# A two-layer trunk on one core: the first units' DMA sums begun with the sub-layer, and each plain tile's weights requested one tile ahead

## The chip, the cores and the metric

The kernel runs on one core of a Trainium2 chip. The metric is device time in microseconds (us) of one execution. The engines are TensorE (PE, matmuls), VectorE (DVE), ScalarE (ACT), GpSimd (POOL) and SyncE (SP, which only issues DMAs here). Each engine works off its own instructions in order; semaphores make one wait for another.

## The reference

A decoder trunk of two layers on a sequence of 512 tokens with 1024 channels. Each layer has a feed-forward part (FFN), a mixer of three groups of heads, a second FFN and a gated per-layer embedding:

```python
for i in range(DEPTH):
    h = rmsnorm(x, g_ffn1_pre[i])
    x = x + 0.5 * rmsnorm(swiglu(h, w1_gate[i], w1_up[i], w1_down[i]), g_ffn1_post[i])
    h = rmsnorm(x, g_mix_pre[i])
    # three head groups from h @ w_in[i], concatenated
    mixed = jnp.concatenate([y_sb, y_mla, y_cv], axis=-1) @ w_out[i]
    x = x + rmsnorm(mixed, g_mix_post[i])
    h = rmsnorm(x, g_ffn2_pre[i])
    x = x + 0.5 * rmsnorm(swiglu(h, w2_gate[i], w2_up[i], w2_down[i]), g_ffn2_post[i])
    h = rmsnorm(x, g_ple_pre[i])
    e = jax.nn.sigmoid(h @ w_ple_gate[i]) * (p[i] @ w_ple_proj[i])
    x = x + rmsnorm(e, g_ple_post[i])

def swiglu(x, w_gate, w_up, w_down):
    return (jax.nn.silu(x @ w_gate) * (x @ w_up)) @ w_down
```

All tensors are 32-bit floats. The FFN's inner width is 2816.

## The kernel before, in words

**Products.** Every 32-bit weight tile is cut into a high half `wh` (a cast by ACT, line 267) and a low half `wl` (a difference, line 268, by DVE or POOL), as the activations are (`xh`, `xl`). A product is three matmuls per 128 rows of depth (lines 283 to 285). Both steps stand in `halves`; `load_raw` (line 258) asks SP for the raw tile. Raw tiles without a tag of their own share four buffers, so a load waits until the halves of an earlier tile have read its buffer.

**An FFN.** The inner width is 22 tiles m. The first four are computed plainly: `order` lists eight products (m, j), j = 0 for gate and 1 for up, called order[0] to order[7] here. Each has 24 matmuls of 512 columns and a PSUM bank whose kind `PLAIN_BANKS = "zsfzzsdf"` names. There is one bank of kind f: order[2] has it first, order[7] next. `activate(m)` reads the banks: line 737 multiplies the gate's by the norm's factor `rb`, line 738 is SiLU on ACT, line 739 multiplies by the up result. The first three products are made together with the sub-layer before (`state.products`), the fourth in `more`, the others in the loop that calls `one`.

**The norm's factor.** It is not known when the products start, so it is applied to their results. `Squares` and `Rstd.add` sum the squares (PE, line 386, into `st`), `rsqrt_cols` (line 366, nine small DVE steps from `r_v` to `rt`) takes the reciprocal root, PE transposes it (line 399), and ACT copies it into `rb` (line 400). `state.behind` is the last of the nine steps; ahead of order[6], `state.row()` puts the transposes into PE's order.

**Units.** The other 18 tiles are `Unit`s: seven products of half the width, from sums of weight blocks, in place of eight. `b11`, `b21` and `b22` are blocks of the weights; `t1` and `t3` are differences of two blocks, stored so that a sum makes them: an SP load of one block, and an accumulating DMA issued by POOL (line 666) that adds the other. They have a buffer of their own kind, as `b21` has. `PREPARE` gives each step of a unit a time in product slots:

```python
PREPARE = (
    ("load", "t1", -18), ("load", "t3", -15), ("load", "b11", -11), ("load", "b21", -10), ("load", "b22", -9), ...
```

`prepare(slot)` issues what is due. The inputs of the units (`fh`, `fl`, lines 611 to 631) are made on ACT and DVE while the plain products run.

**What sets the order.** On PE, in the FFN's loop, the order is the one written. On the other engines a scheduler places each instruction by its priority and a modelled time; `tc.issue_after(x)` keeps what is issued under it behind instruction x. Before, the loads and halves of order[6] and order[7], and all of the units' steps that fall into the loop over the plain products, are under `issue_after(state.behind)`.

Of the kernel before, what the change touches and what calls it, by code (L numbers as in the profile page):

```python
# [24 lines left out]
NF = DFF // P  # L25
# [54 lines left out]
HID_WHOLE = "s" * 2 + "a" * 12 + "s" * 8  # L80
# [5 lines left out]
PLAIN = 4  # L86
# [3 lines left out]
PREPARE = (  # L90
    ("load", "t1", -18), ("load", "t3", -15), ("load", "b11", -11), ("load", "b21", -10), ("load", "b22", -9), ("halve", "b11", -5), ("halve", "b21", -4), ("halve", "t1", -3), ("halve", "t2", -2), ("halve", "b22", 1), ("halve", "t3", 0), ("halve", "t4", 7),
)
# [3 lines left out]
ROW_BEFORE = 6  # L96

TRIG_AT = 2
PLAIN_BANKS = "zsfzzsdf"
BANKS = {"z": 3, "s": 2, "v": 1, "d": 1, "f": 1}  # L100
DENSE = 'zfdszzs'
# [54 lines left out]
def hybrid_trunk(ctx: ExitStack, tc: tile.TileContext, a: dict, out: bass.AP):  # L156
# [7 lines left out]
    ps = ctx.enter_context(tc.tile_pool(name="ps", bufs=1, space=PSUM))  # L164

    def slot(dt=F32, name="s", tag="s"):
        return sp.tile([P, S], dt, tag=tag, name=name, bufs=SLOTS[tag])
# [6 lines left out]
    def bank(name="ps", tag=None):  # L174
        if tag is None:
            tag = dense[0][turn[0] % len(dense[0])]
            turn[0] += 1
        return ps.tile([P, S], F32, tag=tag, name=name, bufs=BANKS[tag])
# [62 lines left out]
    def load_w(src, slabs, cols, on="vv", tag=None):  # L241


        per = S // cols
        return [w for k0 in range(0, slabs, per)
                for w in halves(load_raw(src[:, k0:min(k0 + per, slabs)], cols), on[k0 // per % len(on)], tag)]
# [41 lines left out]
    def start():  # L288
# [5 lines left out]
        def part(k):  # L294
            g = gain(0, "ffn1_pre", k)
            h, lo = xs[k]
            A.activation(out=h, in_=x[k], func=AF.Copy, scale=g)
            V.scalar_tensor_tensor(out=lo, in0=x[k], scalar=g, in1=f(h), op0=ALU.mult, op1=ALU.subtract)
# [11 lines left out]
        for k, c in ((4, 0), (6, 1)):  # L310
# [3 lines left out]
            part(k + 1)  # L314
        first = [(w[t, 0] + w[t, 1], bank("ps", PLAIN_BANKS[t])) for t in range(3)]
        for k in range(NK):
# [54 lines left out]
    class Rstd:  # L371
# [3 lines left out]
        def __init__(self, dim, cols=slice(0, S), tag="v", eps=None, keep=None):  # L375
            self.dim, self.blocks, self.st, self.tag = dim, blocks(cols), None, tag
            self.kw = dict(eps=eps if eps is None else eps[:, cols.start // P:cols.stop // P], keep=keep)
# [35 lines left out]
    def blocks(cols):  # L413
        return [slice(c, c + P) for c in range(cols.start, cols.stop, P)]
# [228 lines left out]
    class Unit:  # L643
# [7 lines left out]
        PAIRS = {"t1": ("b12", "b11"), "t3": ("b12", "b22")}  # L651
        SUMS = {"t2": ("t1", "b22"), "t4": ("t2", "b21")}

        def __init__(self, src, forms, z, tag):
            self.src, self.forms, self.z, self.tag = src, forms, z, tag
            self.raw, self.w, self.bank = {}, {}, {}

        def part(self, n):
# [59 lines left out]
    def ffn(l, idx, state, nxt, xtag="s", early=None):  # L718


        xs = state.xs
        hid, late, banks = [], [], {}
        order = [(m, j) for m in range(PLAIN) for j in range(2)]
        src = a[f"w{idx + 1}_gu"]

        def weights(m, j, on="vv"):
            return load_w(src[l, m, j], NK, P, on)

        def hidden(h):
            if len(hid) < EARLY_HID:  # L730
                hid.append(split(h, HID_HALVES[len(hid)]))
            else:
                late.append(h)

        def activate(m):
            g1 = slot(name="g1", tag=HID_WHOLE[m])
            V.tensor_tensor(out=g1, in0=banks[m, 0], in1=rb, op=ALU.mult)  # L737
            A.activation(out=g1, in_=g1, func=AF.Silu)
            V.tensor_tensor(out=g1, in0=banks[m, 1], in1=g1, op=ALU.mult)
            hidden(g1)  # L740

        def one(m, j):
            w, b = weights(m, j), bank("ps", PLAIN_BANKS[2 * m + j])
            product(b, w, xs)
            banks[m, j] = b

        def more():
            for i in range(FIRST, FIRST + MORE):
                with state.later():
                    w = weights(*order[i])  # L750
                banks[order[i]] = bank("ps", PLAIN_BANKS[i])
                product(banks[order[i]], w, xs)

        if l == 0 and idx == 0:
            first, done = state.first, FIRST
            round_constants()
        else:
            first = [(weights(*t, on), bank("ps", b))
                     for t, on, b in zip(order[:FIRST], (ON_FFN1, ON_FFN2)[idx].split(), PLAIN_BANKS)]
            state.products(first, more)  # L760
            done = FIRST + MORE
        for t, (_, b) in zip(order, first):
            banks[t] = b
        forms = input_forms(l, f"ffn{idx + 1}_pre", xs, xtag)
        units = [Unit(src[l, m], forms, "df"[m % 2], HID_WHOLE[m]) for m in range(PLAIN, NF)]
        todo = sorted((7 * i + t, k, i, n, op) for i in range(len(units)) for k, (op, n, t) in enumerate(PREPARE))

        def prepare(slot):
            while todo and todo[0][0] <= slot:
                _, _, k, form, op = todo.pop(0)  # L770
                getattr(units[k], op)(form)

        rb = None
        with tc.manual_schedule(engines={T.engine}):
            for i in range(done, len(order)):
                if i == ROW_BEFORE:
                    rb = state.row()
                with tc.issue_after(state.behind) if i >= ROW_BEFORE else nullcontext():
                    one(*order[i])
                with tc.issue_after(state.behind):  # L780
                    prepare(8 * (i + 1 - len(order)))
                if rb is not None and i % 2:
                    for m in range(len(hid) + len(late), (i + 1) // 2):
                        activate(m)
            for i in range(len(units) + 1):
                for j, (n, back) in enumerate(PRODUCTS):
                    prepare(7 * i + j)
                    if 0 <= i - back < len(units):
                        u = units[i - back]
                        if n == "p4":  # L790
                            hidden(u.p4(rb))
                        else:
                            getattr(u, n)()
        hid += [split(h, t) for h, t in zip(late, HID_HALVES[EARLY_HID:])]
        turn[0] += 2 * NF + (l + idx > 0)

        sq, ys = Squares(), {}

        def down(m):
            return [w for k0, k1 in DOWN_CHUNKS  # L800
                    for w in load_w(a[f"w{idx + 1}_down"][l, m, :, k0:k1, :], k1 - k0, P)]

        together = [bank() for _ in range(TOGETHER)]
        for k0, k1 in DOWN_CHUNKS:
            for c0 in range(k0, k1, 4):
                c1 = min(c0 + 4, k1)
                ws = [load_w(a[f"w{idx + 1}_down"][l, m, :, c0:c1, :], c1 - c0, P) for m in range(TOGETHER)]
                for k in range(c0, c1):
                    for w, o in zip(ws, together):
                        product(o, w[k - c0:k - c0 + 1], hid[k:k + 1], k == 0, last=k == NF - 1)  # L810
        for m in range(NK - LAST_DOWN):
            if early is not None and m == TRIG_AT:
                early()
            if m < TOGETHER:
                o = together[m]
            else:
                o = bank()
                product(o, down(m), hid)
            ys[m] = slot(name="y")
            sq.add(o)  # L820
            V.tensor_copy(out=ys[m], in_=o)
        last = range(NK - LAST_DOWN, NK)
        w = {m: down(m) for m in last}

        def compute(m, c, tick=lambda: None):
            o = bank()
            product(o, w[m], hid, cols=c, tick=tick)
            return o

        for m in last:  # L830
            ys[m] = slot(name="y")

        def evac(m, c, o):
            V.tensor_copy(out=ys[m][:, c], in_=o[:, c])

        return finish(ys, sq, last, compute, evac, lambda k: half[:, l, idx, k:k + 1], nxt, AT_DOWN, eps=state.eps)
# [484 lines left out]
    state = start()  # L1321
    for l in range(DEPTH):
        state = ffn(l, 0, state, (l, "mix_pre"), xtag="m" if l else "s", early=None if l else trig)
        state = mixer(l, state, (l, "ffn2_pre"))
        state = ffn(l, 1, state, (l, "ple_pre"))
        state = ple(l, state, (l + 1, "ffn1_pre") if l + 1 < DEPTH else None)
# [58 lines left out]
```

## Time and profile before

| what | value |
|---|---|
| median of 3 runs | 2171.48 us (2168.61 to 2175.36) |
| profiled execution | 2170.57 us |
| its span in the profile | 2168.8 us |
| mean granted TensorE clock | 0.977 |
| busy: DVE, ACT, POOL | 1549.2, 1116.5, 509.6 us |

The span is the time from the first to the last instruction that the profile shows. In rows of a timeline stand the start in us, the duration, the engine, the line, the operation, what it writes and reads, how many instructions were joined, and in brackets the idle time ahead of it and what ended that. In rows of windows stand the stretch, its length, then busy time and number of instructions of PE, of its weight loads, of DVE, ACT and POOL, then the granted clock, the DMA engines' busy share and GB/s. Rows of the chain of waits have start, duration and what ran.

### The profile page before, as it was taken

The page shows a single profiled execution, that of the slowest core. Times are in us where ns is not written, and L with a number is a line of the kernel's source. Part 1 is how long each engine was busy: PE and PEld are TensorE (multiplying, and loading weights), DVE is VectorE, ACT ScalarE, POOL GpSimd, SP SyncE. Part 2 cuts the span into 40 slices and gives each one's busy share as a digit, 9 for nine tenths or more (in the row PEclk, how much of TensorE's full clock was granted, in tenths as well). Part 3 has the DMA queues.
Part 4 walks back from the last instruction along what each step waited for, and adds up shares of the span by engine and source line. Part 5 has one row for each costly group of instructions (what it writes and reads, how often), then busy time and mean ns, then how long its engine had stood idle before and what let it go on. Part 6 is the DMA issues. An engine that isn't in the chain of part 4 may idle for free.

```text
span 2168.8 us, 35923 instructions
## 1 busy us (share of the span) xinstructions
PE 2070.1 (95%) x13264; PEld 1883.4 (87%) x13264; DVE 1549.2 (71%) x2851; ACT 1116.5 (51%) x2296; POOL 509.6 (23%) x498
## 2 busy tenths in 40 slices
PE   7999999999998999999979999999999989999996
PEld 6999988887887999888869998888878879998886
DVE  7888654778877788636787786257788778785376
ACT  6555533555555556524555555235455555564243
POOL 3111013126432111003331110031263421110043
PEclk9999999999999999999999999999999899999998
DMA  7677332311115775332247763323111157753322
GB/s 213 173 181 175 86 107 67 95 55 52 53 48 137 188 179 146 102 97 79 78 122 189 178 163 93 100 63 99 55 53 47 45 150 195 175 138 102 97 70 67
DMA packets 139425, 244.73 MB, mean 113 GB/s; under 512 B 15600, under 2 KB 26096, under 8 KB 139248
## 3 DMA queue, kind: packets, MB, share of 16 engines
q1 hardware_dynamic: 117792, 204.00, 30.8%
q0 software_dynamic: 20736, 37.76, 11.0%
q8 instruction: 104, 1.70, 0.3%
q10 hardware_dynamic: 720, 0.67, 0.1%
q14 instruction: 73, 0.60, 0.1%
HBM read 240.27 MB, written 2.10 MB: 112 GB/s over the span
## 4 chain that ended last, share of the span: by engine, by line
PE 81%; DVE 13%; ACT 2%; DMA 2%; issue 1%; POOL 0%; SPq 0%; DVEq 0%; ACTq 0%; POOLq 0%
PE ps L283 10%; PE ps L284 10%; PE ps L285 9%; PE ux L684 6%; PE ux L683 6%; PE ux L682 6%; PE uy L684 3%; PE uy L683 3%; PE uy L682 3%; DVE x L571 3%; PE in L283 2%; PE in L284 2%; PE in L285 2%; DVE xl L467 2%; DVE wl L268 2%; PE uz L684 2%
## 5 line engine op out<-in xcount | busy, mean ns | idle before, releaser
L268 DVE TENSOR_TENSOR wl<-raw,wh 128x512 fp32r<-128x512 f32 (+2 forms) x893 | 601.8, 689 | 416.7 <-ACT wh L267 364.1
L267 ACT CAST wh<-raw 128x512 fp32r<-128x512 f32 (+1 forms) x934 | 548.6, 605 | 606.8 <-PE ps L284 273.9
L441 POOL TENSOR_TENSOR sq<-sq 128x256 f32<-128x256 f32 (+1 forms) x165 | 175.5, 1064 | 798.0 <-ACT sq L431 793.4
L284 PE MATMUL ps<-l,wh 128*128 128x512 f32 (+1 forms) x824 | 302.7, 367 | 0.2 <-DVE l L196 0.2
L285 PE MATMUL ps<-h,wl 128*128 128x512 f32 (+1 forms) x824 | 301.9, 367 | 0.0
L283 PE MATMUL ps<-h,wh 128*128 128x512 f32 (+1 forms) x824 | 300.3, 368 | 0.0
L666 POOL DMA_DIRECT2D raw<-in_w_gu x144 | 125.7, 928 | 634.8 <-DVE wl L268 195.3
L684 PE MATMUL ux<-fh,wl 128*128 128x256 f32 x864 | 244.5, 283 | 0.0
L683 PE MATMUL ux<-fl,wh 128*128 128x256 f32 x864 | 244.5, 283 | 0.0
L682 PE MATMUL ux<-fh,wh 128*128 128x256 f32 x864 | 244.4, 283 | 0.0
L283 PE MATMUL ps<-xh,wh 128*128 128x256 f32 (+1 forms) x536 | 176.7, 353 | 36.5 <-DVE g L737 29.0
L284 PE MATMUL ps<-xl,wh 128*128 128x256 f32 (+1 forms) x536 | 184.0, 351 | 13.0 <-DVE xl L467 12.8
L285 PE MATMUL ps<-xh,wl 128*128 128x256 f32 (+1 forms) x536 | 182.6, 346 | 0.0
L284 PEld LDWEIGHTS ps<-l,wh 128*128 128x128 f32 x824 | 155.6, 189 | 25.7 <-DVE l L196 0.8
L285 PEld LDWEIGHTS ps<-h,wl 128*128 128x128 f32 x824 | 155.4, 189 | 25.1 <-DVE wl L268 0.5
L283 PEld LDWEIGHTS ps<-h,wh 128*128 128x128 f32 x824 | 155.5, 189 | 24.5
L682 PEld LDWEIGHTS ux<-fh,wh 128*128 128x128 f32 x864 | 165.8, 192 | 0.5
L683 PEld LDWEIGHTS ux<-fl,wh 128*128 128x128 f32 x864 | 165.8, 192 | 0.5
L684 PEld LDWEIGHTS ux<-fh,wl 128*128 128x128 f32 x864 | 165.8, 192 | 0.0
L283 PEld LDWEIGHTS ps<-xh,wh 128*128 128x128 f32 x536 | 106.1, 205 | 49.3 <-issue 30.6
L284 PEld LDWEIGHTS ps<-xl,wh 128*128 128x128 f32 x536 | 108.9, 204 | 26.9 <-DVE xl L467 16.7
L285 PEld LDWEIGHTS ps<-xh,wl 128*128 128x128 f32 x536 | 108.8, 204 | 10.8 <-DVE wl L268 0.7
(335 smaller groups left out, 5101.7 us busy)
## 6 DMA issues: line engine op xcount, KB each, us to landing
raw<-in_w_gu SPq DMA_DIRECT2D x424, 256.0 KB, 4.2
raw<-in_w_down SPq DMA_DIRECT2D x160, 256.0 KB, 2.6
raw<-in_w_gu POOLq DMA_DIRECT2D x144, 256.0 KB, 5.2
raw<-in_win_f SPq DMA_DIRECT2D x60, 256.0 KB, 2.7
raw<-in_ple_gate SPq DMA_DIRECT2D x32, 256.0 KB, 2.7
raw<-in_wo_a SPq DMA_DIRECT2D x18, 256.0 KB, 2.7
raw<-in_w_down SPq DMA_DIRECT2D x32, 128.0 KB, 2.2
raw<-in_wo_b SPq DMA_DIRECT2D x12, 256.0 KB, 2.7
```

The source lines that it names most:

```text
L267: A.copy(out=h, in_=raw)
L268: (G if on == "g" else V).tensor_tensor(out=lo, in0=raw, in1=f(h), op=ALU.subtract)
L283: T.matmul(oc, wh, xh[:, cols], start=first and k == 0, stop=False, **kw)
L284: T.matmul(oc, wh, xl[:, cols], start=False, stop=False, **kw)
L285: product.last = T.matmul(oc, wl, xh[:, cols], start=False, stop=last and k == n - 1, **kw)
L441: G.tensor_tensor(out=self.acc[:, c], in0=self.acc[:, c], in1=self.last[:, c], op=ALU.add)
L467: iv = V.scalar_tensor_tensor(out=lo, in0=x[k][:, c], scalar=g, in1=f(h), op0=ALU.mult, op1=ALU.subtract)
L571: V.scalar_tensor_tensor(out=x[k][:, c], in0=ys[k][:, c], scalar=gcol(k), in1=x[k][:, c], op0=ALU.mult, op1=ALU.add)
L666: G.dma_start(out=self.raw[n], in_=self.part(m), accum_op=ALU.add)
L682: T.matmul(o, wh, xh, start=first and k == 0, stop=False, **kw)
L683: T.matmul(o, wh, xl, start=False, stop=False, **kw)
L684: T.matmul(o, wl, xh, start=False, stop=k == 3, **kw)
```

## The change

Three edits, all in `ffn` and `Unit`. The units are made when the sub-layer starts, before its first plain products; for the first two (`AHEAD`) t1 and t3 are loaded at once, four SP loads and four accumulating DMAs of POOL, and taken out of the list of things due. In the loop, the weights (loads and halves) of the next plain tile are requested before the product of this one. And these requests are no longer held behind `state.behind`; the units' other steps still are. A unit gets its inputs (`forms`) later. No computation is added or removed. Lines 98 to 655 of before stand two lower in the changed file, the lines of `activate` too.

```diff
+AHEAD = 2
...
-        def __init__(self, src, forms, z, tag):
-            self.src, self.forms, self.z, self.tag = src, forms, z, tag
+        def __init__(self, src, z, tag):
+            self.src, self.z, self.tag = src, z, tag
...
-        def one(m, j):
-            w, b = weights(m, j), bank("ps", PLAIN_BANKS[2 * m + j])
+        def one(m, j, w):
+            b = bank("ps", PLAIN_BANKS[2 * m + j])
             product(b, w, xs)
             banks[m, j] = b
...
+        units = [Unit(src[l, m], "df"[m % 2], HID_WHOLE[m]) for m in range(PLAIN, NF)]
+        todo = sorted((7 * i + t, k, i, n, op) for i in range(len(units)) for k, (op, n, t) in enumerate(PREPARE)
+                      if op != "load" or i >= AHEAD or n not in ("t1", "t3"))
+        for u in units[:AHEAD]:
+            u.load("t1")
+            u.load("t3")
...
-        units = [Unit(src[l, m], forms, "df"[m % 2], HID_WHOLE[m]) for m in range(PLAIN, NF)]
-        todo = sorted((7 * i + t, k, i, n, op) for i in range(len(units)) for k, (op, n, t) in enumerate(PREPARE))
...
+        for u in units:
+            u.forms = forms
         rb = None
         with tc.manual_schedule(engines={T.engine}):
+            ws = [weights(*order[done])]
             for i in range(done, len(order)):
                 if i == ROW_BEFORE:
                     rb = state.row()
-                with tc.issue_after(state.behind) if i >= ROW_BEFORE else nullcontext():
-                    one(*order[i])
+                if i + 1 < len(order):
+                    ws.append(weights(*order[i + 1]))
+                one(*order[i], ws[i - done])
                 with tc.issue_after(state.behind):
                     prepare(8 * (i + 1 - len(order)))
```

Three places show how instructions move; all are in layer 0's second FFN.

SP, the loads around order[6] and order[7], before. raw_7753 and raw_7759 are order[6]'s, raw_7796 and raw_7800 are b11 and b22 of the first unit, raw_7743 to raw_7868 the first blocks of t1 and t3 of three units, raw_7805 and raw_7811 order[7]'s, raw_7798 is b21:

```order
L258 DMA raw_7753<-in_w2_gu 128x512
L258 DMA raw_7759<-in_w2_gu 128x512
L258 DMA raw_7796<-in_w2_gu 128x512
L258 DMA raw_7800<-in_w2_gu 128x512
L258 DMA raw_7743<-in_w2_gu 128x512
...
L258 DMA raw_7868<-in_w2_gu 128x512
L258 DMA raw_7805<-in_w2_gu 128x512
L258 DMA raw_7811<-in_w2_gu 128x512
L258 DMA raw_7798<-in_w2_gu 128x512
L258 DMA raw_7855<-in_w2_gu 128x512
```

SP with the change. raw_7302 to raw_7311 are t1 and t3 of two units, raw_7730 and raw_7736 order[6]'s, raw_7774 and raw_7780 order[7]'s, raw_7846 and raw_7868 t1 and t3 of the third unit, raw_7811 and raw_7815 are b11 and b22, raw_7813 is b21:

```order
L260 DMA raw_7302<-in_w2_gu 128x512
...
L260 DMA raw_7311<-in_w2_gu 128x512
...
L260 DMA raw_7730<-in_w2_gu 128x512
L260 DMA raw_7736<-in_w2_gu 128x512
L260 DMA raw_7774<-in_w2_gu 128x512
L260 DMA raw_7780<-in_w2_gu 128x512
L260 DMA raw_7846<-in_w2_gu 128x512
L260 DMA raw_7868<-in_w2_gu 128x512
L260 DMA raw_7811<-in_w2_gu 128x512
L260 DMA raw_7815<-in_w2_gu 128x512
...
L260 DMA raw_7940<-in_w2_gu 128x512
L260 DMA raw_7813<-in_w2_gu 128x512
```

The four loads have gone up by some ten rows, ahead of the plain tiles, order[7]'s stand straight behind order[6]'s, and b11, b22 and b21 come after them; b21 is behind raw_7940, which waits for b11's halves.

DVE, from the root's first steps to the op that reads order[2]'s bank f (ps_7340, last row), before. wl_7756 and wl_7762 are order[6]'s low halves, wl_7808 and wl_7814 order[7]'s, wl_7843 b11's, wl_7852 b21's, wl_7858 t1's:

```order
L366 TENSOR_SCALAR r_v_7586<-st_7580 128x4
...
L366 TENSOR_SCALAR r_y0_7587<-r_v_7586 128x4
...
L366 SCALAR_TENSOR_TENSOR rt_7585<-r_w_7590,r_z_7589 128x4
L268 TENSOR_TENSOR wl_7756<-raw_7753,wh_7755 128x512
L268 TENSOR_TENSOR wl_7762<-raw_7759,wh_7761 128x512
L268 TENSOR_TENSOR wl_7808<-raw_7805,wh_7807 128x512
L737 TENSOR_TENSOR g1_7875<-ps_7314,rb_7746 128x512
...
L268 TENSOR_TENSOR wl_7814<-raw_7811,wh_7813 128x512
L268 TENSOR_TENSOR wl_7843<-raw_7796,wh_7842 128x512
...
L268 TENSOR_TENSOR wl_7852<-raw_7798,wh_7851 128x512
L268 TENSOR_TENSOR wl_7858<-raw_7743,wh_7857 128x512
...
L737 TENSOR_TENSOR g1_7883<-ps_7340,rb_7746 128x512
```

DVE with the change. wl_7733 and wl_7739 are order[6]'s, wl_7777 and wl_7783 order[7]'s, wl_7843, wl_7852 and wl_7858 are b11's, b21's and t1's again; rt_7597 is the root's last step, and ps_7352 order[2]'s bank:

```order
L270 TENSOR_TENSOR wl_7733<-raw_7730,wh_7732 128x512
...
L270 TENSOR_TENSOR wl_7739<-raw_7736,wh_7738 128x512
L270 TENSOR_TENSOR wl_7777<-raw_7774,wh_7776 128x512
L368 TENSOR_SCALAR r_v_7598<-st_7592 128x4
L270 TENSOR_TENSOR wl_7783<-raw_7780,wh_7782 128x512
...
L368 SCALAR_TENSOR_TENSOR rt_7597<-r_w_7602,r_z_7601 128x4
L270 TENSOR_TENSOR wl_7843<-raw_7811,wh_7842 128x512
L739 TENSOR_TENSOR g1_7891<-ps_7705,rb_7767 128x512
L739 TENSOR_TENSOR g1_7875<-ps_7326,rb_7767 128x512
...
L270 TENSOR_TENSOR wl_7852<-raw_7813,wh_7851 128x512
L270 TENSOR_TENSOR wl_7858<-raw_7302,wh_7857 128x512
...
L739 TENSOR_TENSOR g1_7883<-ps_7352,rb_7767 128x512
```

The four low halves of order[6] and order[7] have moved from behind the root to ahead of its end, and two of `activate`'s first multiplications ahead of b21's half; ahead of the one that reads order[2]'s bank stand b21's and t1's halves.

POOL, before: the mixer's last low half (kl_4796), its squares (sq), and then the accumulating DMAs of the units:

```order
L187 TENSOR_TENSOR kl_4796<-kf_6481,kh_4795 64x512
L441 TENSOR_TENSOR sq_6964<-sq_6964,sq_6966 128x256
...
L441 TENSOR_TENSOR sq_7248<-sq_7248,sq_7250 128x256
...
L666 DMA raw_7743<-in_w2_gu 128x512
L666 DMA raw_7790<-in_w2_gu 128x512
L666 DMA raw_7793<-in_w2_gu 128x512
L666 DMA raw_7802<-in_w2_gu 128x512
L666 DMA raw_7846<-in_w2_gu 128x512
```

POOL with the change:

```order
L189 TENSOR_TENSOR kl_4796<-kf_6481,kh_4795 64x512
L668 DMA raw_7302<-in_w2_gu 128x512
L668 DMA raw_7305<-in_w2_gu 128x512
L668 DMA raw_7308<-in_w2_gu 128x512
L668 DMA raw_7311<-in_w2_gu 128x512
L443 TENSOR_TENSOR sq_6964<-sq_6964,sq_6966 128x256
...
L443 TENSOR_TENSOR sq_7248<-sq_7248,sq_7250 128x256
...
L668 DMA raw_7846<-in_w2_gu 128x512
```

Four of the accumulating DMAs now stand ahead of the mixer's last squares instead of behind them.

## The prediction

> **What bounds the kernel now.** I read the shares of the engines first, then what TensorE (PE) waits for, then PE's rows in order of time, and at each long gap the chain of waits.
>
> ```profile
> PE 2070.1 (95%) x13264; PEld 1883.4 (87%) x13264; DVE 1549.2 (71%) x2851; ACT 1116.5 (51%) x2296; POOL 509.6 (23%) x498
> ```
>
> PE is busy 95% of 2168.8 us, and the change neither adds nor takes away a matmul. So it can only win the rest: places where PE stands, and places where PE runs slowly. The view of waits has one PE entry that is four single waits, and PE's rows in order of time give them:
>
> ```profile
> PE ps L283 <- DVE g L737: 29.0, 4, 8.9
> ...
> 55.02 0.77 PE L283 MATMUL ps<-xh,wh 128*128 128x512 f32 x1 [4.24 <-DVE g L737]
> 692.60 0.76 PE L283 MATMUL ps<-xh,wh 128*128 128x512 f32 x1 [8.89 <-DVE g L737]
> 1134.01 0.77 PE L283 MATMUL ps<-xh,wh 128*128 128x512 f32 x1 [7.26 <-DVE g L737]
> 1771.96 0.76 PE L283 MATMUL ps<-xh,wh 128*128 128x512 f32 x1 [8.59 <-DVE g L737]
> ```
>
> There is one per FFN; I call them stalls 0 to 3. All four stand before the last plain product, order[7], which goes to bank f, held until line 737 has read order[2]'s result. They sum to 28.98 us. Each also costs clock afterwards:
>
> ```profile
> 700.46 0.39 PE L285 MATMUL ps<-xh,wl 128*128 128x512 f32 x1
> 700.69 0.28 PE L682 MATMUL ux<-xh,wh 128*128 128x256 f32 x1
> 62.80 0.28 PE L682 MATMUL ux<-xh,wh 128*128 128x256 f32 x1
> 1141.62 0.28 PE L682 MATMUL ux<-xh,wh 128*128 128x256 f32 x1
> 1779.73 0.28 PE L682 MATMUL ux<-xh,wh 128*128 128x256 f32 x1
> 694.00:696.00 2.00, 2.00 (x6) 1.60 (x5) 2.00 (x5) 1.78 (x4) 0.00 (x0) 0.50 0.00 0
> ```
>
> The granted clock (third number from the right) is 0.50 behind the stall. At the end of the product the matmuls start 0.23 us apart again (700.46 to 700.69); at that pace the 24 matmuls of order[7] need 5.52. They took 8.09 in stall 1 (692.60 to 700.69), and 7.78, 7.61 and 7.77 in stalls 0, 2 and 3: 2.6 + 2.3 + 2.1 + 2.2 = 9.2 us more. All that the change can win here is therefore 29.0 + 9.2 = 38.2 us.
>
> Who ends stall 1? The chain of waits there:
>
> ```profile
> 665.15 0.60 DVE wl L268
> ...
> 666.15 0.60 DVE wl L268
> ...
> 675.57 1.22 DVE wl L268 x2
> 676.86 8.76 DMA raw<-in_w_gu
> 685.64 1.14 ACT wh L267 x2
> 686.80 1.28 ACT L738
> 688.10 0.64 ACT g L738
> ...
> 691.85 0.61 DVE g L737
> ```
>
> Halves of order[6], queued behind the norm's reciprocal root, run at 675.57 and free two raw buffers; order[7]'s weights go into those, and the second landed 8.76 us later. Its cast stands on ScalarE (ACT) ahead of the SiLU work, its difference on VectorE (DVE) ahead of line 737. So PE does not wait for order[7]'s weights as such, but for DVE and ACT work queued behind them. Stall 3 repeats this chain with one number changed, and stalls 0 and 2 have the same links:
>
> ```profile
> 1756.43 8.55 DMA raw<-in_w_gu
> ```
>
> **The change part by part, on stall 1.** *Weights one tile ahead.* order[7]'s loads now follow order[6]'s on SyncE (SP) and wait for order[5]'s halves, 665.15 and 666.15 above. They go out at about 665.8 and 666.8, where b11 and b22 went; before, it was 676.24:
>
> ```profile
> 665.78 2.27 SPq L258 DMA_DIRECT2D raw<-in_w_gu  x4
> 676.24 2.16 SPq L258 DMA_DIRECT2D raw<-in_w_gu  x3
> 677.64 0.60 PE L399 MATMUL rb<-ident,rt 128*128 128x128 f32 x4
> raw<-in_w_gu SPq DMA_DIRECT2D x424, 256.0 KB, 4.2
> raw<-in_w_down SPq DMA_DIRECT2D x160, 256.0 KB, 2.6
> ```
>
> They land by 671 to 672 (median 4.2), while DVE still makes input forms: hidden. The price: four halves, two of order[6] and two of order[7], now stand ahead of the root instead of behind it. 4 x 0.60 = 2.4 us, so the root is done at about 678.0 instead of 675.57. Before, PE's transposes of it ran at 677.64; now they wait 0.4 us.
>
> *What is late next.* On DVE the op that frees bank f (line 739 of the changed file, whose lines here are two higher) is now behind b11's and b21's halves. b21's load stands on SP behind a load that waits for b11's halves, and those follow the root (678.0 + 0.6). b21 goes out near 679.4; before it was the third of the issues at 676.24. With the median of 4.2 it lands at 683.6; cast 0.6, two differences 1.2, line 198 0.6, line 739 0.6, 0.1 to PE: order[7] starts at 686.7. The SiLU branch is ready sooner: transposes and copy to 679.3, then a table load of 1.28 and two SiLUs of 0.64 to 681.9. Against 692.60 that is 5.9 us won. PE was free at 692.60 - 8.89 = 683.7, now 684.1, so 2.6 us of stall stay. The landing is bounded by 2.6 (w_down's median, a quieter stretch) and 8.76 (order[7]'s own before): order[7] at 685.1 or 691.3, 7.5 or 1.3 won. I take 4.2, the same tensor on the same queue.
>
> *The DMA sums first.* Per FFN four SP loads and four accumulating DMAs of POOL leave the crowded stretch. In stages 1 and 3 they are put ahead of the mixer's last squares on POOL, which stands idle there, four issues at some 0.93 us being 3.7 us:
>
> ```profile
> 619.53 2.37 POOL L441 TENSOR_TENSOR sq<-sq 128x256 f32<-128x256 f32 x3 [40.38 <-ACT sq L431]
> L666 POOL DMA_DIRECT2D raw<-in_w_gu x144 | 125.7, 928 | 634.8 <-DVE wl L268 195.3
> 640.00:660.00 20.00, 18.50 (x125) 17.26 (x125) 19.35 (x40) 12.81 (x32) 12.96 (x16) 0.91 0.08 27
> ```
>
> Hidden by those 40 us; without that cover it would be 3.7. The last window before the crowded stretch has a DMA share of 0.08, so the loads find room.
>
> *Stall 3* has stage 1's order; its chain was 0.2 us shorter from load to product: 5.7 won, 2.5 left.
>
> *Stall 2.* Here PE's transposes came later than the root:
>
> ```profile
> 1117.54 1.22 DVE wl L268 x2
> 1120.68 0.60 PE L399 MATMUL rb<-ident,rt 128*128 128x128 f32 x4
> 1067.70 1.01 PE L386 MATMUL st<-con,sq 128*128 128x1 f32 x4 [1.47 <-ACT sq L522]
> ```
>
> Root at 1117.5 + 2.4 = 1119.9, no wait for PE; b11's halves to 1120.5, b21 out at 1121.4, landed 1125.6, then 3.1 us of the same steps: 1128.7 against 1134.01, 5.3 won. PE is free at 1126.75, so 2.0 us stay. The four POOL issues sit among the squares of the sub-layer before, 3.7 us in all; PE's sums over the squares waited until 1067.70 for a square of ACT anyway. I count nothing; the ends are 0 and 3.7 lost.
>
> *Stall 0.* The added loads go ahead of order[3]'s in the first 15 us, and DVE does the moved halves beside POOL's squares:
>
> ```profile
> 24.00:32.00 8.00, 8.00 (x37) 6.64 (x36) 6.36 (x8) 7.48 (x15) 8.00 (x7) 1.00 1.00 268
> 34.42 6.74 POOL L441 TENSOR_TENSOR sq<-sq 128x512 f32<-128x512 f32 x4
> 36.80 1.50 DVE L187 TENSOR_TENSOR fl<-xg,fh 128x512 fp32r<-128x512 f32 x1 [0.20 <-ACT fh L616]
> 44.42 0.16 DVE L366 SCALAR_TENSOR_TENSOR rt<-r_w,r_z 128x4 f32<-128x4 f32 x1
> ```
>
> The root moves from 44.4 to about 45.5, b21 goes out at 46.7, lands at 50.9, and six steps (cast, two differences, lines 741, 674, 198 and 739: 4.2 us) end at 55.1 against 55.02: nothing won. Bounds: four halves at 1.5 instead of 0.6 beside POOL lose 3.6; no wait at all wins 4.2 and 2.3 of clock. The row at 36.80 (1.50, where a difference at 665.15 took 0.60) says that the contention is real. The page "SBUF — State Buffer" of the Trainium skill, section "Who interferes with whom", has it as a rule: VectorE's two-input operations contend with GpSimd's reads. By that rule the moved halves cost the 3.6, and the sum below would be 16.9.
>
> *Clock.* Stalls of 2.6, 2.0 and 2.5 us stay. Do such short ones cost the clock? Two rows of before, with the stretch behind each:
>
> ```profile
> 1006.76 0.38 PE L284 MATMUL ps<-xl,wh 128*128 128x256 f32 x1 [2.18 <-DVE xl L467]
> 1008.00:1012.00 4.00, 3.78 (x23) 3.13 (x23) 4.00 (x7) 1.57 (x4) 2.07 (x2) 1.00 0.37 117
> 1089.26 0.43 PE L399 MATMUL rb<-ident,rt 128*128 128x128 f32 x2 [2.93 <-DVE rt L366]
> 1090.00:1094.00 4.00, 4.00 (x23) 3.97 (x22) 3.83 (x5) 2.42 (x7) 3.82 (x5) 0.58 0.31 107
> ```
>
> 2.18 kept it, 2.93 lost it. I count half of 2.6 + 2.1 + 2.2 = 6.9, that is 3.5; the ends are 0 and 6.9. The Trainium skill ("TensorE: Matmul & The Clock Gate", section "Why this matters for your kernels") warns of gaps over about 3 us; by that rule all three stalls would keep the clock, and the sum would be 3.5 higher. The 2.93 row speaks against so sharp a bound.
>
> *Sum:* 0 + 5.9 + 5.3 + 5.7 + 3.5 = 20.4 us. The profiled execution took 2170.57 (span 2168.8), 0.9 below the median of 2171.48: 2170.57 - 20.4 = 2150.2.
>
> **The rivals.**
> *Stalls gone.* b21 lands in 2.6 us and the clock holds: 3 x 1.6 + 3.5 more is 28.7 us, 2142; if also stall 0 and the rest vanish, the full 38.2, 2132. For it: fewer POOL sums are in flight. Against it: b21 cannot be asked for before b11's halves.
> *b21 takes order[7]'s place.* If b21 needs 8.76 us too, 1.3 + 0.7 + 1.1 = 3.1 us are won and the clock is lost: 2167.5, no change that a measurement would tell. For it: six SP loads are queued within some 8 us there. Against it: most of the POOL sums that shared those 8.76 us have gone.
> *The root waits for order[7]'s weights: slower.* In DVE's queue the second half of order[7] now stands in the middle of the root's steps, so a late landing holds the root, PE's transposes ahead of order[6], and all SiLU work. By the rows above that half's turn comes at about 674.0, with a cast of 0.6 ahead of it, so each microsecond that the weights land after 673.4 costs one. It decides from a landing of 12.5 us after 666.8, where the 5.9 are used up; at 16 us each of three stalls loses 3.5, with stall 0's 3.6 some 14 us: 2185. For it: DMA share 1.00 in the start-up. Against it: 0.08 just ahead of the others.
> *The change does nothing:* if SP's queue held order[7]'s loads anyway. order[5]'s halves at 665.15 and 666.15 speak against that.
>
> **How the numbers follow.** No change is told from a change within 0.3%, 6.5 us: faster is below 2165, slower above 2178. Forecast (2146 to 2160) 0.48; stalls gone (2132 to 2146) 0.25; b21 takes the place (2160 to 2169) 0.15, of which a third would still be below 2165; nothing 0.04; slower 0.08. So faster 0.78, same 0.14, slower 0.08. The range 2135 to 2169 leaves out the slower case, no change and the outermost part of the stalls gone, together less than 0.2; the likeliest case alone is 2146 to 2160.
>
> **What would show it.** Right: order[7]'s loads in front of the root, its product some 6 us earlier after a stall of 1 to 3 us that ends with line 739, and a b21 transfer in the chain there; PE's transposes waiting under 1 us in stages 1 and 3; POOL's early issues done before 619; stall 0 within 3 us of 4.24. Wrong: transposes waiting several microseconds for the root; PE waits in the mixer's or the last sub-layer's tail that were not there; order[3] late in the first 30 us; a clock of 0.50 after every stall.

## The result, and the profile after

| | before | with the change | ratio, 95% interval |
|---|---|---|---|
| first comparison, median | 2172.32 us (4 runs) | 2146.09 us (2142.72 to 2149.54, 4 runs) | 0.988 (0.9857 to 0.9904) |
| the change again, another call | 2168.21 us (11 runs) | 2150.68 us (2145.29 to 2155.07, 6 runs) | 0.9909 (0.9893 to 0.9926) |

The change wins 17 to 26 us. (Of the last kernel of the experiments one execution in five took 7861 us at a granted clock of 0.476; the ratios leave it out.) The profiled execution took 2149.54 us, the slowest of its four, with a span of 2147.7 against 2168.8: 21.1 us less in the two profiles. PE's busy time moved by 3.7 us only, from 2070.1 to 2066.4, so most of it is waiting:

```profile
PE 2066.4 (96%) x13264; PEld 1879.5 (88%) x13264; DVE 1552.6 (72%) x2851; ACT 1117.2 (52%) x2296; POOL 507.4 (24%) x498
PE ps L285 <- DVE g L739: 5.6, 3, 2.3
54.27 0.77 PE L285 MATMUL ps<-xh,wh 128*128 128x512 f32 x1 [2.91 <-ACT wh L269]
688.03 0.49 PE L285 MATMUL ps<-xh,wh 128*128 128x512 f32 x1 [2.16 <-DVE g L739]
1125.99 0.47 PE L285 MATMUL ps<-xh,wh 128*128 128x512 f32 x1 [2.31 <-DVE g L739]
1753.89 0.47 PE L285 MATMUL ps<-xh,wh 128*128 128x512 f32 x1 [1.11 <-DVE g L739]
```

These are the engine shares, the entry of the view of waits that was 29.0 us in four times, and the first matmul of order[7] in each FFN. The stalls were 4.24, 8.89, 7.26 and 8.59; they are 2.91, 2.16, 2.31 and 1.11, 20.5 us less. (The cast named at 54.27 is only the last event; the program has this matmul wait for line 739's read of bank f, which ran at 53.45.)

SP's issues of order[7]'s weights, the transposes of the root, and the link that now stands in the chain of waits of stalls 1 to 3, b21's transfer:

```profile
667.49 0.33 SPq L260 DMA_DIRECT2D raw<-in_w_gu  x1
668.48 0.33 SPq L260 DMA_DIRECT2D raw<-in_w_gu  x1
679.75 0.62 PE L401 MATMUL rb<-ident,rt 128*128 128x128 f32 x4 [0.47 <-DVE rt L368]
680.98 3.74 DMA raw<-in_w_gu
1118.47 4.20 DMA raw<-in_w_gu
1747.53 3.04 DMA raw<-in_w_gu
```

The weights go out at 667.5 and 668.5, 8.4 to 8.8 us earlier than before, in a trace whose PE ran 1.5 us later by then (the same matmul starts at 667.51, and before at 666.02). They are no longer in the chain. PE waits 0.47 us for the root.

Something was also lost. In the tail of layer 0's last sub-layer, PE's sums over the squares wait for POOL. The first seven rows are of the change, the last three of the same place before:

```profile
1062.35 0.61 PE L388 MATMUL st<-con,sq 128*128 128x1 f32 x4 [2.16 <-POOL sq L443]
1065.23 1.01 PE L388 MATMUL st<-con,sq 128*128 128x1 f32 x4 [1.47 <-ACT sq L524]
1056.43 3.41 DVE L1302 TENSOR_TENSOR pp<-pp,g 128x512 f32<-128x512 f32 x1 [0.75 <-ACT g L1301]
1056.18 1.78 POOL L668 DMA_DIRECT2D raw<-in_w_gu  x2
1057.33 1.95 POOL L443 TENSOR_TENSOR sq<-sq 128x512 f32<-128x512 f32 x1
1058.58 2.43 POOL L668 DMA_DIRECT2D raw<-in_w_gu  x2
1066.00:1070.00 4.00, 4.00 (x20) 4.00 (x20) 1.53 (x10) 0.42 (x1) 0.00 (x0) 0.50 0.32 102
1064.84 0.61 PE L386 MATMUL st<-con,sq 128*128 128x1 f32 x4
1061.07 1.61 DVE L1293 TENSOR_TENSOR pp<-pp,g 128x512 f32<-128x512 f32 x1 [0.75 <-ACT g L1292]
1067.00:1073.00 6.00, 5.29 (x25) 5.30 (x26) 2.50 (x12) 1.14 (x3) 1.27 (x1) 0.50 0.28 89
```

The wait of 2.16 us at 1062.35 is new; the one at 1065.23 was there before (at 1067.70). The four DMA issues stand on POOL among its squares, and while they run, VectorE's product took 3.41 us and POOL's square 1.95; before, at the same place, they took 1.61 and 1.29. Behind the wait the granted clock is 0.50, but so it was before. I call the time by which a matmul runs earlier than the same matmul before its lead. From the transposes at 1014.25 (before: 1018.91) to the sums at 1065.23 (before: 1067.70) the lead falls from 4.7 to 2.5 us: this place costs 2.2 us. (At 1001.28, before 1006.76, the lead was still 5.5. A wait of 2.11 us there is followed by a clock of 0.56 in the change; before, one of 2.18 us kept 1.00.) A wait of 2.15 to 2.17 us at this place stands in all five profiles with sums issued among those squares, and in none of the eight without.

### The profile page after: what moved, and what is told of

Its sections match the earlier page's. It is cut to its first block, busy times and chain, and to the rows that moved or that the text cites. A ratio compares the mean times of both kernels' runs of the same rounds, so it can differ in the third digit from the quotient of the medians.

```text
span 2147.7 us, 35941 instructions
## 1 busy us (share of the span) xinstructions
PE 2066.4 (96%) x13264; PEld 1879.5 (88%) x13264; DVE 1552.6 (72%) x2851; ACT 1117.2 (52%) x2296; POOL 507.4 (24%) x498
## 4 chain that ended last, share of the span: by engine, by line
PE 81%; DVE 13%; ACT 2%; issue 2%; DMA 1%; POOL 0%; SPq 0%; DVEq 0%; ACTq 0%; POOLq 0%
PE ps L286 9%; PE ps L285 9%; PE ps L287 9%; PE ux L686 6%; PE ux L685 6%; PE ux L684 6%; PE uy L686 3%; PE uy L685 3%; PE uy L684 3%; DVE x L573 2%; PE in L286 2%; PE in L287 2%; PE in L285 2%; DVE wl L270 2%; DVE xl L469 2%; PE uz L686 2%
```

## The experiments

Two theories. A: order[7] waited for bank f, that is for DVE and ACT work queued ahead of the op that reads order[2]'s result; the weights moved ahead took most of that away, the early sums nearly nothing. B: the early sums are needed, since they make the room on the DMA engines in which weights and b21 land. Each kernel was timed against the kernel before on the same chip; "stalls" are PE's waits in front of order[7], FFN by FFN.

| kernel | median us | ratio to before, 95% | stalls 0 to 3, us |
|---|---|---|---|
| the change | 2146.1 | 0.9880 (0.9857 to 0.9904) | 2.9, 2.2, 2.3, 1.1 |
| the change again | 2150.7 | 0.9909 (0.9893 to 0.9926) | 2.6, 3.0, 2.3, 2.2 |
| weights only | 2163.9 | 0.9976 (0.9964 to 0.9987) | none, 7.0, 6.1, 6.1 |
| sums only | 2155.5 | 0.9936 (0.9916 to 0.9956) | 3.7, 4.6, 2.0, 4.7 |
| no early sums in layer 1's first FFN | 2151.6 | 0.9922 (0.9900 to 0.9943) | 2.6, 2.6, 6.6, 1.8 |
| before, two bank letters exchanged | 2154.7 | 0.9930 (0.9912 to 0.9947) | none, 0.9, 1.9, 1.7 |
| the change, letters exchanged | 2137.7 | 0.9845 (0.9828 to 0.9861) | none |
| the change, first b21 early | 2142.0 | 0.9869 (0.9849 to 0.9889) | 2.3, 1.1, 1.1, 1.1 |
| the change, layer 1's sums behind the squares | 2148.5 | 0.9897 (0.9879 to 0.9916) | 2.3, 2.7, 0.5, 2.1 |
| the last with letters exchanged | 2134.1 | 0.9834 (0.9817 to 0.9852) | none |
| the same again | 2133.1 | 0.9836 (0.9822 to 0.9851) | none |
| the same, none early in the first FFN | 2136.7 | 0.9854 (0.9837 to 0.9872) | none |

**One half of the change at a time.** Weights only:

```diff
-AHEAD = 2
+AHEAD = 0
```

> The change without the early DMA sums: each plain tile's weights requested one tile ahead, t1 and t3 of every unit loaded when they were loaded before. Theory A (order[7] waited for DVE and ACT work queued ahead of the op that frees bank f, and moving the weights ahead of the root took most of it away; the early sums are nearly idle weight, and cost about 3 us in the tail of layer 0's last sub-layer, where PE waited 2.16 us for a POOL square): 2142 to 2149 us, the wait at 1062 gone, stalls of 1 to 4 us in front of order[7]. Theory B (the early sums made the room on the DMA engines without which the weights and b21 land late): stalls of 5 us and more, 2156 to 2166 us.

Sums only:

```diff
-            ws = [weights(*order[done])]
...
-                if i + 1 < len(order):
-                    ws.append(weights(*order[i + 1]))
-                one(*order[i], ws[i - done])
+                with tc.issue_after(state.behind) if i >= ROW_BEFORE else nullcontext():
+                    one(*order[i], weights(*order[i]))
```

> The change without the earlier weights: t1 and t3 of the first two units loaded at the start of the sub-layer, order[6]'s and order[7]'s weights requested behind the root as before. Theory A: order[7]'s loads still go out behind the root, their casts and halves still stand ahead of the op that frees bank f; the landing may shrink from 8.8 to some 5 us, 3 us of new wait in the tail of layer 0's last sub-layer: 2160 to 2172 us. Theory B: landing near 4 us and bank f free 4 to 5 us earlier in three stalls, clock kept in part: 2148 to 2158 us.

Theory A failed on both. The weights alone win 0.24%, the sums alone 0.64%, that is 4.6 and 13.0 us by the medians; with the weights alone stall 0 is gone, and the other three are 1.2 to 2.5 us shorter. With the weights only, in the chain of waits of stall 1 b21 has taken order[7]'s place; below it the DMA queues of that kernel in the stretch 666 to 686, and then those of the change:

```profile
674.55 8.84 DMA raw<-in_w_gu
686.70 0.76 PE L285 MATMUL ps<-xh,wh 128*128 128x512 f32 x1 [6.99 <-DVE g L739]
q1 hardware_dynamic: 1749, 3.18, 47.1%
q0 software_dynamic: 864, 1.57, 44.8%
raw<-in_w_gu SPq DMA_DIRECT2D x7, 256.0 KB, 7.2
```

```profile
q1 hardware_dynamic: 1872, 3.41, 52.7%
q0 software_dynamic: 288, 0.52, 15.6%
raw<-in_w_gu SPq DMA_DIRECT2D x13, 256.0 KB, 3.7
```

The columns are packets, MB and share of the 16 engines' time. POOL's sums take nearly as much engine time for 1.57 MB as SP's loads for 3.18. With four of the six gone from the stretch, the median landing of an SP load falls from 7.2 to 3.7 us, and b21's from 8.84 to 3.74, although SP itself moves no less (3.41 MB). With the sums only, order[7]'s own load needs 4.57 us instead of 8.76, and the rest of the old chain stays:

```profile
674.39 4.57 DMA raw<-in_w_gu
685.95 0.77 PE L285 MATMUL ps<-xh,wh 128*128 128x512 f32 x1 [4.58 <-DVE g L739]
```

So the sums shorten whichever load is in the chain, and the weights put a shorter chain in its place. The sums are the larger part, and theory B holds for the landing. That each half needs the other is not shown: 4.6 and 13.0 add up to 17.6 us, and the change wins 17 to 26.

**The loss in layer 0's last tail.** First without early sums at that one place:

```diff
+        ahead = 0 if (l, idx) == (1, 0) else AHEAD
...
```

> The change, but in layer 1's first FFN no sum is loaded early (the other three FFNs unchanged), so POOL issues no accumulating DMA among the squares of the sub-layer before. Theory A: the wait of 2.16 us for a POOL square at 1062 and the half clock behind it go, about 3 us: 2141 to 2144 against 2146 for the change, if stall 2 stays near 2.3. Rival (the new wait is hidden by the wait for ACT's square 3 us later, and the 3 us are run-to-run variation): 2146 as the change.

```profile
1052.60 1.60 DVE L1303 TENSOR_TENSOR pp<-pp,g 128x512 f32<-128x512 f32 x1 [0.76 <-ACT g L1302]
1059.21 0.61 PE L388 MATMUL st<-con,sq 128*128 128x1 f32 x4 [1.47 <-ACT sq L524]
1111.81 8.47 DMA raw<-in_w_gu
1123.60 0.76 PE L285 MATMUL ps<-xh,wh 128*128 128x512 f32 x1 [6.60 <-DVE g L739]
```

The same product takes 1.60 us instead of 3.41, and the wait for POOL's square is gone, so the four issues were its cause. But stall 2 grows from 2.31 to 6.60, with b21 at 8.47 us: what is won in the tail is more than given back, neither of the two expectations came true, and the median is no better than the change's. Then the four issues behind the squares of the sub-layer's entry, on POOL, with their first loads where they were:

```diff
...
+            with tc.issue_after(Squares.done.ins):
+                for u in units[:AHEAD]:
+                    u.gather("t1")
+                    u.gather("t3")
```

> The change, but in layer 1's first FFN the four accumulating DMAs stand on POOL behind the squares of the sub-layer's entry; their first loads go out as in the change. Theory A (these four issues slow POOL's and VectorE's work in the tail of the sub-layer before, and all that they buy is room for b21 at 1118): the 2.16 us wait at 1062 goes, the four are done well before 1118 and stall 2 stays at 2 to 3 us; 3 us below the change, ratio 0.9865. Rival (the later they come, the more they collide with order[5]'s to order[7]'s loads): stall 2 grows by 3 to 4 us as without early sums, ratio 0.989 to 0.990.

```profile
1095.77 3.56 POOL L673 DMA_DIRECT2D raw<-in_w_gu  x4
1099.22 8.90 DMA raw<-in_w_gu
1108.85 0.69 DVE L270 TENSOR_TENSOR wl<-raw,wh 128x512 fp32r<-128x512 f32 x1 [1.35 <-ACT wh L269]
1112.95 0.62 PE L401 MATMUL rb<-ident,rt 128*128 128x128 f32 x4 [2.94 <-DVE rt L368]
```

The wait at 1062 went, and stall 2 with it (0.5). In their place PE waits 2.94 us for the root, because DVE stands idle before a half of order[7] that is queued between the root's steps; it waits there for order[7]'s second load, which needed 8.90 us beside the four sums (in the change it went out at 1106.32 and was cast at 1110.38, 4.1 us later at most). The median of 2148.5 is not to be told from the change. The ratio is the rival's (0.989 to 0.990), and so is the collision, but the wait came at the root and not in stall 2. Two things follow. The sums are what makes the loads beside them late, for here only they were moved back. And the prediction's slower rival, a root that waits for order[7]'s weights, is real, if small.

**What is left of the stalls.** b21 asked for at the start of the sub-layer:

```diff
...
+        units[0].load("b21")
```

> The change with the first unit's b21 requested at the start of the sub-layer too, in all four FFNs. Theory A (VectorE's queue ahead of the bank's op sets the time; b21's landing leaves VectorE idle for 1.1 us only, and t1's halves move up into the room): the stalls shrink by under 1 us each, ratio 0.986 to 0.988. Rival (the landing of b21, 3 to 4 us in the chain of each stall, is what is left): it goes out of the chain, the stalls shrink by 2 us or vanish and the clock is kept: ratio 0.982 to 0.984.

```profile
676.22 1.90 DVE L270 TENSOR_TENSOR wl<-raw,wh 128x512 fp32r<-128x512 f32 x3
683.66 0.47 PE L285 MATMUL ps<-xh,wh 128*128 128x512 f32 x1 [1.14 <-DVE g L739]
```

The transfer leaves the chain, as the rival said, but the stalls only fall to 1.1 us (2.3 at the start), and the ratio of 0.9869 lies in the range of theory A of this run: from the three halves at 676.22 until the op that reads the bank, at 682.83, DVE has no idle time. The interval overlaps that of the first comparison, so b21 early is not shown to be faster than the change. Then the two bank letters, on the kernel before and on the change:

```diff
-PLAIN_BANKS = "zsfzzsdf"
+PLAIN_BANKS = "fszzzsdf"
```

> The kernel before with two letters exchanged in PLAIN_BANKS (order[0] gets bank f, order[2] a z), so that order[7] waits for the op that reads order[0]'s bank, the first that DVE makes, and no longer for order[2]'s; weights and sums as before. Theory A (the wait is for the bank, not for the weights): order[7] starts when its first half is there, near 684.7 in stall 1; stalls 0 to 3 shrink to 0 to 1.5 us, the clock is kept: 2134 to 2142 us. Rival (the weights' landing itself is the limit, the bank only named because it came last): stalls of 4 to 6 us, 2158 to 2166 us.

On the kernel before, stall 1 is 0.94 us instead of 8.89, with order[7]'s weights as late as they were: the wait was for the bank. But only 14 us are won of the 38.2, a median between the two expectations, for the units then wait for their own late loads and copies:

```profile
679.83 0.50 PE L283 MATMUL ps<-xh,wh 128*128 128x512 f32 x1 [0.94 <-DVE g L737]
689.22 0.36 PE L682 MATMUL uz<-xh,wh 128*128 128x256 f32 x1 [2.22 <-ACT wh L267]
693.09 0.58 PE L682 MATMUL ux<-fh,wh 128*128 128x256 f32 x1 [1.41 <-ACT g L689]
```

> The change with two letters exchanged in PLAIN_BANKS (order[0] gets bank f, order[2] a z), so that order[7] waits for the op that reads order[0]'s bank. Theory A (what is left of the four stalls is the place of that op behind b21's and t1's halves on VectorE): it runs near 681.6 in stall 1, before PE is free at 685.9; the stalls of 2.9, 2.2, 2.3 and 1.1 us and the half clock behind two of them, 4.9 us, go: some 13 us below the change, ratio to before 0.982. Rival (as with the two letters alone, the wait moves into the units: their casts and first bank copies are late): 3 to 6 us below the change, ratio 0.985 to 0.987, new waits in lines 684 to 686.

On the change, all four stalls are gone, and nothing comes in their place: order[0]'s bank is read at 677.89 there, the second of two, and PE begins order[7] without a gap at 682.52:

```profile
677.89 1.29 DVE L739 TENSOR_TENSOR g<-ps,rb 128x512 f32<-128x512 f32 x2 [0.46 <-ACT rb L402]
682.52 0.39 PE L285 MATMUL ps<-xh,wh 128*128 128x512 f32 x1
```

The ratio of 0.9845 lies between the two expectations (0.982, and 0.985 to 0.987): the stalls went as theory A said, but the wait of 2.15 us in layer 0's last tail and one of 1.23 us ahead of order[3] in the first FFN stayed.

**The version that beats both.** Letters exchanged and layer 1's sums behind the squares:

> The change with both edits: the two bank letters exchanged and layer 1's four accumulating DMAs behind the entry's squares. If both theories A hold the gains add: 13 + 3 us below the change, ratio 0.980 to 0.981. If the exchange only moves the wait into the units: 0.984 to 0.986.

> The change with the two bank letters exchanged and layer 1's four accumulating DMAs behind the entry's squares, once more: 0.982 to 0.985, below the change in the same call by 10 to 14 us.

2134.1 and 2133.1: 0.9834 and 0.9836, 1.6% below before and some 12 to 18 us below the change, and between the two expectations of the first of these runs. Against the letters alone (0.9845) the intervals overlap, so the second edit is not shown to help. Beside it ran the change again:

> The change itself once more, beside the next two: the measure of what one execution differs from another. All theories: ratio 0.987 to 0.989; in its profile the same four stalls in front of order[7], 1 to 3 us each; whether the clock is lost behind those of 2 to 3 us may come out otherwise than in the first profile, by some 2 us each.

Its four stalls are as expected, its ratio of 0.9909 is not (0.987 to 0.989). One reason stands in its profile, the slowest of its six: in layer 1's mixer the granted clock is 0.50 or 0.51 in three stretches (at 1481, 1519 and 1587) where the first profile has 1.00, and over that mixer it loses 4.2 us against the first profile.

And without early sums in the very first FFN:

> As the one before, but no sums begun early in the very first FFN, where loads, constants and the first weights share the DMA engines. Theory A (the early sums delay order[3]'s weights and the last inputs there: waits of 1.0 us at 16.9 and 1.25 us at 27.0 in the change's profile, which the kernel before did not have): both go, and with bank f read early nothing waits for b21 at 54: 1 to 3 us below. Rival (without the early sums b21 and t1 come late and the units wait): the same or up to 4 us above.

```profile
45.06 0.16 DVE L368 SCALAR_TENSOR_TENSOR rt<-r_w,r_z 128x4 f32<-128x4 f32 x1
45.32 1.09 PE L401 MATMUL rb<-ident,rt 128*128 128x128 f32 x4 [3.60 <-issue]
```

The wait ahead of order[3], 1.28 and 1.25 us in the two runs just before, went. (The wait of 1.0 us at 16.9 was in the first profile of the change; these two runs did not have it.) At the transposes a wait of 3.60 us came that the profile puts down to nothing it shows ("issue"; 3.43 in the weights-only kernel, 1.88 before). The rows of DVE tell what it is: the root's last step ends at 45.22, 0.1 us ahead of the transposes, as it does in the weights-only kernel (45.28 and 45.38) and before (44.58 and 44.69). So PE waits for the root. DVE has no idle time from 37.67 until the root is done, with the moved halves in that queue; before, it stood idle for 1.13 us ahead of the root's first step. The medians are 2136.7 and 2133.1, with intervals that overlap: nothing is gained, within the rival's range but by another wait than it named.

## Why the prediction was right, point by point

- **What bounds it:** right. The four waits shrank from 29.0 to 8.5 us. The kernel before with its letters exchanged shows directly that they were waits for bank f.
- **Order[7]'s loads:** forecast at 665.8 and 666.8, came at 667.5 and 668.5 in a trace that ran 1.5 us later by then.
- **The root and the transposes:** 0.4 us forecast, 0.47 measured in stall 1, 0.26 in stall 2. The root, forecast at 678.0, was done at 679.6, 678.1 without the 1.5.
- **POOL's early issues:** in stage 1 they ran from 611.20 to 614.76, ahead of the squares, and cost nothing there, as forecast.
- **What is late next:** right. b21 is the link, with 3.74, 4.20 and 3.04 us for the 4.2 taken. Order[7] was forecast at 686.7 and came at 688.03, 686.5 without the 1.5. Stalls of 2.6, 2.0 and 2.5 us were to stay; 2.16, 2.31 and 1.11 did, and in the second profile of the change 2.95, 2.26 and 2.15.
- **Stall 0:** "nothing won" was right for the stretch, not in its parts: the stall fell from 4.24 to 2.91, but waits of 1.02 and 1.25 us appeared at 16.9 and 27.0, in the stretch where the added loads stand ahead of order[3]'s (0.21 and 1.25 in the second profile). The units start at 62.63 against 62.80. The 3.6 us that the other end put on the moved halves did not come: a half at 36.93, beside POOL's squares, took 1.78 us, and the four from 39.23 on took 0.68 each, since the last of those squares ended at 38.15. (20.4 less 3.6 is 16.8, not 16.9.)
- **Stall 2, mis-sized:** the four POOL issues among the squares were counted at nothing, with 3.7 us as the other end. They cost 2.2. The row at 1067.70 was read as cover, but it shows a wait of 1.47 us for ACT's square that comes behind the new one and is still there: it hid nothing. The issues also slowed VectorE, which the step left out for this place though it had a row of such contention in stall 0. This wait and the late order[3] are two of the signs that the prediction had named for being wrong.
- **Clock:** half of 6.9 us was counted as won. In the first profile stalls 2 and 3 kept the clock and stall 1 lost it: order[7] took 5.56, 5.56 and 7.17 us, and 5.2 of the 6.9 were won. In the second, 3.6 were won; a stall of 2.26 kept it and one of 2.15 lost it:

```profile
1123.04 0.47 PE L285 MATMUL ps<-xh,wh 128*128 128x512 f32 x1 [2.26 <-DVE g L739]
1125.00:1128.00 3.00, 3.00 (x15) 2.48 (x14) 3.00 (x6) 2.28 (x5) 0.00 (x0) 1.00 0.12 41
1757.06 0.47 PE L285 MATMUL ps<-xh,wh 128*128 128x512 f32 x1 [2.15 <-DVE g L739]
1757.00:1760.00 3.00, 2.94 (x8) 2.34 (x9) 3.00 (x6) 3.00 (x6) 0.00 (x0) 0.59 0.00 0
```

  So half was right for the second and low for the first, and a bound by length alone does not hold: in the kernel without early sums in layer 1's first FFN a stall of 1.80 us lost the clock (0.54 behind it) and one of 2.61 kept it (1.00). Such differences, stall 3 at 1.1 in one execution and 2.2 in another, and the clock in layer 1's mixer, set the two profiles of the change apart. That they also set apart its two medians, 4.6 us, is likely but not shown.
- **The sum:** 20.4 forecast, 21.1 between the two profiles. From the transposes to the units the lead grows by 7.0, 6.6 and 9.4 us in stalls 1 to 3, some 23 in all, and 0.2 is won in the first FFN; 2.2 are lost in the tail. That the sum fits so well is partly luck: stall 3 won more than its 5.7 and its share of the clock, because b21 landed in 3.04 us and the clock was kept, and this paid for the tail. The forecast of 2150.2 stands 4.1 us above the first median and 0.5 below the second.
- **The early sums, not priced:** the sum took 4.2 us for b21 as the median of this tensor's loads, and of the early sums it counted only what they cost; that sums had gone from the stretch was named among the rivals alone. But the value hangs on them. For the weights without the sums the same steps would have given nearly the same forecast, and that kernel won 4.6 us, with b21 at 8.84 us. This is the rival in which b21 takes order[7]'s place (8.76 assumed). It won 1.2 us in stage 1, where the rival had 1.3; that its median, 2163.9, is near the rival's 2167.5 is in part chance, since stall 0 went as well, which the rival had not counted.

## What to carry to other kernels

Before moving loads, ask which buffer the waiting engine really waits for and who frees it last: here exchanging two bank letters removed the wait that a reordering of loads only shortened, and the two together were best. When a load in the chain lands late, look at what else is in flight: here the summing transfers cost about twice the engine time per byte, and with four of six out of the stretch the median landing of the loads beside them fell from 7.2 to 3.7 us. A step that is moved under "idle" time of one engine can still slow its neighbour there; read the durations in that stretch, not the busy share alone.

## What the runs showed of the hardware that was not expected

- Accumulating DMAs issued by POOL took 44.8% of the DMA engines' time for 1.57 MB where plain loads took 47.1% for 3.18 MB in the same 20 us: 1.9 times as much per byte.
- A VectorE product of 512 columns took 3.41 us beside POOL's DMA issues and a square, and 1.61 and 1.60 in the two kernels shown that have no issues there.
- The granted clock after a stall of about 2 us went either way: 1.00 behind stalls of 2.26, 2.31 and 2.61 us, and 0.5 to 0.6 behind stalls of 1.80, 2.15 and 2.16 us, all in front of the same product.
